# A two-layer matrix product by Strassen's scheme: block 0's second product moved ahead of block 1's first, partial outputs fetched from GpSimd's queue into output tiles, and a looped fallback

## The chip, the cores and the metric

The kernel runs on one core of one Trainium2 chip. The metric is device time in microseconds (us). The five engines of the core are named as the profile names them: PE (TensorE, the matrix products; PEld is its weight load), DVE (VectorE), ACT (ScalarE), POOL (GpSimd) and SP (SyncE). Each runs its own list of instructions in order and waits on semaphores for the others. SP, ACT and POOL issue DMAs: SP's go to hardware queue q1, ACT's to q10, POOL's to the software queue q0. All of them share 16 DMA engines.

## What is computed

```python
batch, m, k, h, n = 16, 512, 768, 3072, 768
y = np.matmul(x, w1) + b1        # x: 8192 rows of 768; w1: 768 x 3072
y = np.maximum(y, 0)
return np.matmul(y, w2)          # w2: 3072 x 768
```

All inputs and the output are float32 in DRAM.

## The kernel before

**Tiling.** The 8192 rows are cut into NSB = 8 blocks of 1024 rows, and the 3072 hidden columns into NCH = 2 halves. That gives NIT = 16 blocks of work, `it` = 0 to 15: blocks 0 to 7 are all rows with the first half of the hidden columns, blocks 8 to 15 all rows again with the second half. Each block has a first product (x times w1, bias, ReLU, giving y in f16) and a second product (y times w2). Both are done by Strassen's scheme in Winograd's form: seven products of half size instead of eight, on operands that are sums of quarters. DVE forms these sums: `sums_x` (three instructions, L230, L233, L237), `sums_w` (four, L190), `sums_y` (three, L291, L293, L295). Block 0's first product alone is done plainly (`first_plain`), since the sums of x and w1 do not exist yet.

**Groups and steps.** The work is a list of groups that is written by hand in `run` and then sorted by a key, so that the steps of neighbouring groups alternate. A group ("p1", 0, t) is block 0's plain first product for hidden tile t, four steps of six matmuls. A group ("m1", it, t) is the first product of block `it` for tile t of six: seven steps p1, p2, p6, p5, p7, p3, p4 of three matmuls of 128x512 (L336). A group ("m2", it, j) is the second product for 128-row tile j of four: seven steps of the same names, six matmuls of 128x384 each (L413). In a group the accumulator `a` is used on and on: step p6 adds onto it after ACT or DVE has copied it, p4 after DVE has taken p7 (L346 and L418 are the additions on DVE, L342 and L424 the copies on ACT).

Before the change the list is: block 0's six p1 groups; then for each block, the first two m1 groups of the next block, the four m2 groups of this one, and the last four m1 groups of the next. So two m1 groups of block 1 stand ahead of block 0's first m2 group.

**What hangs on the steps.** After each step `after` issues side work: loads of x and weights, transposes, sums, squares for a range check, saves to DRAM and fetches from it. Since every engine runs in program order, the place in this list is the place in each engine's queue. But an instruction is held only by its own engine's earlier ones and by its own data: a DMA hooked to a late step can start early when its queue is empty and its data are ready.

**x.** Block 0's rows come as float32 in eight DMAs from SP and ACT (`load_x_first`, L260), are turned on PE (L270) and copied to f16 by DVE and ACT (L277, L275). Later blocks come as f16 from POOL (`load_x`, L210) in two halves into the two buffers of the pool `raw`, are turned by DMA transposes on SP (`transpose_x`, L216), summed on DVE, and saved with their sums to DRAM (`save_x`, L240, 2688 KB) for blocks 8 to 15, which fetch them (`fetch_x`, L244). ACT squares the raw rows for the check (`square_x`, L222) and writes the squares over the rows. The tile of x has two buffers, so block 2's x takes the place of block 0's.

**Weights.** w1 comes by L172 and w2 by L179, both on POOL. `first_plain` sums each w1 tile at once. The six w2 tiles are summed in p1 groups 4 and 5 and in the first two m1 groups of block 1. The second half of w2 is loaded, summed and saved one tile a block in blocks 0 to 5.

**Output.** Blocks 0 to 7 store partial outputs; blocks 8 to 15 fetch them (`fetch_part`, L398, on SP, into a tile `pr` of the pool `raw`), add them and store again (L460 and L465, on SP). The two row halves of a group go to separate tiles `o1` and `o2`, two buffers each.

**Range check and fallback.** `out_of_range` (L486 to L512) reduces the squares to one count after block 11, which every engine reads into a register at once. At the end a branch (L669) skips `general_path`, a plain version of the whole computation, written out in full.

Of the kernel before, what the change touches and what calls it, by code (L numbers as in the profile page):

```python
# [27 lines left out]
def general_path(ctx, tc, xf, w1, b1, w2, of):  # L28

    nc = tc.nc  # L30
    M, K = xf.shape
    H, N = w2.shape
    KS, HS, MB = K // P, H // P, 512
# [7 lines left out]
    nc.sync.dma_start(out=b1_sb, in_=b1.rearrange("(t p) -> p t", p=P))  # L41
    nc.gpsimd.dma_start(out=w1_sb, in_=w1.rearrange("(t p) h -> p t h", p=P))
    nc.gpsimd.dma_start(out=w2_sb, in_=w2.rearrange("(t p) n -> p t n", p=P))
    xl_pool = ctx.enter_context(tc.tile_pool(name="gxl", bufs=2))
    xt_pool = ctx.enter_context(tc.tile_pool(name="gxt", bufs=2))
    yt_pool = ctx.enter_context(tc.tile_pool(name="gyt", bufs=2))
    o_pool = ctx.enter_context(tc.tile_pool(name="go", bufs=4))
    ps_t = ctx.enter_context(tc.tile_pool(name="gpt", bufs=2, space=PSUM))
    ps_1 = ctx.enter_context(tc.tile_pool(name="gp1", bufs=2, space=PSUM))
    ps_2 = ctx.enter_context(tc.tile_pool(name="gp2", bufs=4, space=PSUM))  # L50
    for m0 in range(0, M, MB):
        xt = xt_pool.tile([P, KS, MB], BF16, name="gxt")
        for r in range(0, MB, P):
            xl = xl_pool.tile([P, K], BF16, name="gxl")
            nc.gpsimd.dma_start(out=xl, in_=xf[m0 + r:m0 + r + P, :])
            pt = ps_t.tile([P, KS, P], BF16, name="gpt")
            for k in range(KS):
                nc.tensor.transpose(pt[:, k, :], xl[:, k * P:(k + 1) * P], ident)
            nc.vector.tensor_copy(out=xt[:, :, r:r + P], in_=pt)
        yt = yt_pool.tile([P, HS, MB], BF16, name="gyt")  # L60
        for h in range(HS):
            ps = ps_1.tile([P, MB], FP32, name="gp1")
# [3 lines left out]
            nc.scalar.activation(out=yt[:, h, :], in_=ps, func=ACTF.Relu,  # L66
                                 bias=b1_sb[:, h:h + 1])
        for r in range(0, MB, P):
            o = o_pool.tile([P, N], FP32, name="go")
            for j in range(2):  # L70
                ps = ps_2.tile([P, NF], FP32, name="gp2")
                for h in range(HS):
                    nc.tensor.matmul(ps, lhsT=yt[:, h, r:r + P],
                                     rhs=w2_sb[:, h, j * NF:(j + 1) * NF],
                                     start=(h == 0), stop=(h == HS - 1))
                nc.vector.tensor_copy(out=o[:, j * NF:(j + 1) * NF], in_=ps)
            nc.sync.dma_start(out=of[m0 + r:m0 + r + P, :], in_=o)


class Strassen:  # L80
# [66 lines left out]
    def constants(self):  # L147
        nc = self.nc
        HS = self.H // P
        self.ident = self.const.tile([P, P], FP32, name="ident")  # L150
        make_identity(nc, self.ident)
        self.b1_sb = self.const.tile([P, HS], FP32, name="b1_sb")
        self.b1y = self.const.tile([P, HS], FP32, name="b1y")

        self.xstat = self.const.tile([P, self.M // P], FP32, name="xstat")
        self.w1stat = self.const.tile([P, self.NCH * self.TP], FP32, name="w1stat")
        self.w2stat = self.const.tile([P, self.NCH * self.TP], FP32, name="w2stat")

    def bias(self):
        nc = self.nc  # L160
        nc.sync.dma_start(out=self.b1_sb, in_=self.b1.rearrange("(t p) -> p t", p=P))
        nc.vector.tensor_scalar(out=self.b1y, in0=self.b1_sb, scalar1=YS, scalar2=None,
                                op0=ALU.mult)

# [21 lines left out]

    def sums_w(self, w):
        for o, i, j in ((self.T3, self.B12, self.B22), (self.T1, self.B12, self.B11),
                        (self.T2, self.B22, self.T1), (self.T4, self.B21, self.T2)):
            self.nc.vector.tensor_tensor(out=w[:, o], in0=w[:, i], in1=w[:, j],  # L190
                                         op=ALU.subtract)

    def stat_w(self, stat, c, t, w):

        i = c * self.TP + t
# [3 lines left out]
                                  accum_out=stat[:, i:i + 1])  # L199
# [5 lines left out]
    def load_x(self, it):  # L205
        m0 = it * 2 * self.MH
        for half in range(2):
# [11 lines left out]
    def square_x(self, it, half, s, rows=None):  # L219
        i = (it * 2 + half) * 4 + s  # L220
        rows = self.raw[half][:, s, :] if rows is None else rows
        self.nc.scalar.activation(out=rows, in_=rows, func=ACTF.Square,  # L222
                                  accum_out=self.xstat[:, i:i + 1])
# [22 lines left out]
    def load_x_first(self):  # L246

        self.first_rows = []
        for half in range(2):
            if half == 0:  # L250
                tiles = [self.o_pool.tile([P, 1, self.N], FP32, name="xf", tag=f"o{1 + s // 2}")
                         for s in range(4)]
            else:
                two = [self.raw_pool.tile([P, 2, self.N], FP32, name="xf", tag="raw")
                       for _ in range(2)]
                tiles = [two[s // 2][:, s % 2:s % 2 + 1] for s in range(4)]
            for s, xr in enumerate(tiles):
                r = half * self.MH + s * P
                q = self.nc.sync if s % 2 else self.nc.scalar
                q.dma_start(out=xr[:, 0, :], in_=self.xf[r:r + P, :])  # L260
                self.first_rows.append(xr[:, 0, :])

    def transpose_x_first(self, half):
        nc = self.nc
        for s in range(4):
            rows = self.first_rows[half * 4 + s]
            for a in range(2):
                ps = (self.pa, self.pc)[a].tile([P, 3, P], FP32, name="ac"[a], tag="ac"[a])
                for k in range(3):
                    nc.tensor.transpose(ps[:, k, :],  # L270
                                        rows[:, (3 * a + k) * P:(3 * a + k + 1) * P],
                                        self.ident)
# [24 lines left out]
    def first_plain(self, t):  # L297
# [96 lines left out]
    def fetch_part(self, it, j):  # L394

        pr = self.raw_pool.tile([P, 2, self.N], FP32, name="pr", tag="raw")
        for half in range(2):
            self.nc.sync.dma_start(out=pr[:, half, :], in_=self.rows_of(it, j, half))  # L398
        self.part[it, j] = pr

    def second(self, it, j):
# [5 lines left out]
        pr = self.part.pop((it, j), None)  # L407
# [13 lines left out]
        def take(o, ps, half, col):  # L421

            if pr is None:
                nc.scalar.activation(out=o, in_=ps, func=ACTF.Copy, scale=inv)  # L424
            else:
                add(o, ps, pr[:, half, col * NH:(col + 1) * NH])

        def copy(name, ps, half, col):
            g[name] = self.s_tile(name)[:, 0:NH]
            take(g[name], ps, half, col)  # L430

# [5 lines left out]
        def p2():  # L437
            g["b"] = self.pb.tile([P, self.MH], FP32, name="b")[:, 0:NH]
            mm(g["b"], self.A12, self.B21, True)
            g["o1"] = self.o_pool.tile([P, self.N], FP32, name="o1")  # L440
            add(g["o1"][:, 0:NH], g["b"], g["s1"])
# [10 lines left out]
        def p7():  # L452
            mm(g["a"], self.S3, self.T3, False)
            g["o2"] = self.o_pool.tile([P, self.N], FP32, name="o2")
            add(g["o2"][:, NH:], g["a"], g["s5"])

        def p3():
            mm(g["c"], self.S4, self.B22, False)
            add(g["o1"][:, NH:], g["c"], g["s2"])
            nc.sync.dma_start(out=self.rows_of(it, j, 0), in_=g["o1"])  # L460

        def p4():
            mm(g["a"], self.A22, self.T4, False)
            take(g["o2"][:, 0:NH], g["a"], 1, 0)
            nc.sync.dma_start(out=self.rows_of(it, j, 1), in_=g["o2"])  # L465

        return [p1, p2, p6, p5, p7, p3, p4]


    def out_of_range(self):  # L470
# [6 lines left out]
        nw = self.NCH * self.TP  # L477
        nx, nb = self.M // P, self.H // P
        ones = self.const.tile([P, P], FP32, name="ones")
        nc.vector.memset(ones, 1.0)  # L480
        n = 2 * nw + nx + nb
        ok = self.const.tile([P, n], FP32, name="ok")
        low = self.const.tile([P, n], FP32, name="low")
        val = self.const.tile([P, n], FP32, name="val")

        nc.vector.tensor_copy(out=val[:, 0:nw], in_=self.w1stat)  # L486
        nc.vector.tensor_copy(out=val[:, nw:2 * nw], in_=self.w2stat)
        nc.vector.tensor_copy(out=val[:, 2 * nw:2 * nw + nx], in_=self.xstat)
        nc.vector.tensor_tensor(out=val[:, 2 * nw + nx:], in0=self.b1_sb, in1=self.b1_sb,
                                op=ALU.mult)  # L490
        ps = self.pb.tile([P, self.MH], FP32, name="b")
        nc.tensor.matmul(ps[:, 0:2 * nw], lhsT=ones, rhs=val[:, 0:2 * nw], start=True,
                         stop=True)
        nc.vector.tensor_copy(out=val[:, 0:2 * nw], in_=ps[:, 0:2 * nw])
        at = 0
        for width, hi, lo in ((nw, W1_HI, W1_LO), (nw, W2_HI, W2_LO), (nx, X_HI, X_LO),
                              (nb, B_HI, 0.0)):
            v = val[:, at:at + width]
# [203 lines left out]
```

## Time and profile before

| what | value |
|---|---|
| runs | 968.33, 970.03, 971.53 us; median 970.03 |
| profiled execution, its own time | 971.14 us |
| its span in the profile | 969.3 us |
| mean granted clock of PE | 0.978 |
| busy: PE, DVE, ACT, POOL | 899.5, 598.2, 407.2, 47.6 us |
| moved by DMA | 163.35 MB, mean 169 GB/s |
| HBM read, written | 95.37 MB, 76.48 MB |

The span is cut into 40 slices of 24.2 us for the digits of the page. A line of waits reads: who waited, for whom, the total in us, how many times, the longest. A line of a timeline reads: start and duration in us, engine, line, operation, what it writes and reads, its shape, how many were merged, and in brackets the idle time before it and what ended that. A line of a group ends in: busy us, mean ns of one, idle us before, and who ended most of that. A line of stretches reads: the stretch, its length, then busy us and instructions of each engine that has any, the granted clock, the share of the DMA engines and their GB/s. PE's matmuls are pipelined: the next starts before the one before it ends, so the work is counted by their spacing.

### The profile page before, as it was taken

Reading aid. Unit: us, or ns where it says so; the run is one execution under the profiler, and the core shown is the slowest. Engines: PE = TensorE matmul, PEld = TensorE weight load, DVE = VectorE, ACT = ScalarE, POOL = GpSimd, SP = SyncE. Lnnn points to the kernel's source line nnn. Section 1 sums busy time; section 2 is a strip of 40 time slices with the busy share of each in tenths; the row PEclk is TensorE's granted clock in tenths of the full one; section 3 lists DMA queues with packets and bytes.
Section 4 is the critical chain, followed back from the end, with each engine's and each line's share of the span. In section 5 each row is a group of like instructions: output and inputs, shape, how many; then the busy total and the mean of one; then the engine's idle time right before and its main releaser. Section 6 shows DMA issues by size and latency. Waiting matters only on the chain. (4 is left out here: it accounts for less than half of the span.)

```text
span 969.3 us, 12976 instructions
## 1 busy us (share of the span) xinstructions
PE 899.5 (93%) x4774; PEld 472.6 (49%) x4774; DVE 598.2 (62%) x1114; ACT 407.2 (42%) x697; POOL 47.6 (5%) x68
## 2 busy tenths in 40 slices
PE   4926999999999999999999999999998999998995
PEld 2502545545454555545454545545454554544543
DVE  0519276584857566583856768485765848576563
ACT  1733447758555545553525136153502405041220
POOL 4220000100000000010200000000000000000000
PEclk9968899999999999999999999999999999999998
DMA  9395895785858594754837443534443245331514
GB/s 228 57 189 162 222 289 109 211 188 131 254 128 261 108 309 97 242 155 126 165 113 291 189 180 131 214 145 163 149 181 144 114 180 191 134 131 66 195 49 151
DMA packets 113528, 163.35 MB, mean 169 GB/s; under 512 B 70960, under 2 KB 84272, under 8 KB 111408
## 3 DMA queue, kind: packets, MB, share of 16 engines
q1 hardware_dynamic: 80144, 140.41, 41.9%
q0 software_dynamic: 32736, 20.45, 15.7%
q10 hardware_dynamic: 576, 1.57, 0.4%
q8 instruction: 39, 0.64, 0.3%
q14 instruction: 33, 0.27, 0.1%
HBM read 95.37 MB, written 76.48 MB: 177 GB/s over the span
## 5 line engine op out<-in xcount | busy, mean ns | idle before, releaser
L413 PEld LDWEIGHTS <-y 128*128 128x128 f16 x2688 | 264.2, 98 | 205.2 <-issue 23.0
L336 PEld LDWEIGHTS <-w1s 128*128 128x128 f16 x1890 | 186.0, 98 | 226.9 <-issue 18.2
L413 PE MATMUL a<-w2s,y 128*128 128x384 f16 x1536 | 278.3, 328 | 18.7 <-DVE s L418 11.1
L336 PE MATMUL a<-x,w1s 128*128 128x512 f16 x1080 | 270.9, 382 | 5.7 <-ACT s L342 4.3
L342 ACT ACTIVATE s<-a,b1y 128x512 f32<-128x512 f32 x180 | 123.7, 687 | 332.6 <-PE a L336 326.5
L336 PE MATMUL c<-x,w1s 128*128 128x512 f16 x540 | 146.6, 380 | 0.9 <-DVE flag L510 0.7
L413 PE MATMUL c<-w2s,y 128*128 128x384 f16 x768 | 147.3, 328 | 0.0
L418 DVE SCALAR_TENSOR_TENSOR o<-a,s 128x384 f32<-128x384 f32 x64 | 35.4, 553 | 84.8 <-PE a L413 60.7
L346 DVE SCALAR_TENSOR_TENSOR y<-a,s 128x512 f16<-128x512 f32 x90 | 61.6, 684 | 35.9 <-ACT s L342 31.9
L291 DVE TENSOR_TENSOR y<-y 128x512 f16<-128x512 f16 x96 | 40.8, 425 | 63.3 <-ACT y L380 53.3
L380 ACT ACTIVATE y<-a,b1y 128x512 f16<-128x512 f32 x90 | 61.8, 687 | 31.9 <-PE a L336 31.9
L336 PE MATMUL b<-x,w1s 128*128 128x512 f16 x270 | 73.5, 381 | 0.0
L413 PE MATMUL b<-w2s,y 128*128 128x384 f16 x384 | 72.9, 326 | 0.0
L418 DVE SCALAR_TENSOR_TENSOR s<-a,pr 128x384 f32<-128x384 f32 x64 | 35.3, 551 | 57.7 <-DMA pr<-out_dram 50.0
L293 DVE TENSOR_TENSOR y<-y 128x1024 f16<-128x1024 f16 x96 | 66.4, 692 | 3.3
L342 ACT ACTIVATE s<-c,b1y 128x512 f32<-128x512 f32 x90 | 61.8, 687 | 12.9 <-PE c L336 12.9
L424 ACT ACTIVATE s<-a 128x384 f32<-128x384 f32 x64 | 31.2, 487 | 78.4 <-PE a L413 73.7
L346 DVE SCALAR_TENSOR_TENSOR y<-b,s 128x512 f16<-128x512 f32 x90 | 61.5, 684 | 2.5 <-PE b L336 1.6
L346 DVE SCALAR_TENSOR_TENSOR y<-c,s 128x512 f16<-128x512 f32 x90 | 61.3, 681 | 0.5
L222 ACT ACTIVATE xn<-xn 128x768 f16<-128x768 f16 x56 | 46.8, 837 | 22.9 <-DMA x<-xn 22.8
L375 DVE TENSOR_SCALAR y<-y 128x1536 f16<-128x1536 f16 x90 | 50.4, 560 | 3.1
L418 DVE SCALAR_TENSOR_TENSOR o<-b,s 128x384 f32<-128x384 f32 x64 | 35.4, 553 | 20.3 <-PE b L413 10.2
(59 smaller groups left out, 413.4 us busy)
## 6 DMA issues: line engine op xcount, KB each, us to landing
out_dram<-o SPq DMA_DIRECT2D x128, 384.0 KB, 2.6
pr<-out_dram SPq DMA_DIRECT2D x64, 384.0 KB, 4.1
xd<-x SPq DMA_DIRECT2D x8, 2688.0 KB, 12.6
x<-xd SPq DMA_DIRECT2D x8, 2688.0 KB, 9.3
xn<-in_x_dram POOLq DMA_DIRECT2D x14, 768.0 KB, 10.2
w1s<-in_w_dram POOLq DMA_DIRECT2D x24, 192.0 KB, 8.3
w2d<-w2t SPq DMA_DIRECT2D x6, 672.0 KB, 6.3
w2s<-w2d SPq DMA_DIRECT2D x6, 672.0 KB, 7.3
```

What stands on the lines that cost most here:

```text
L222: self.nc.scalar.activation(out=rows, in_=rows, func=ACTF.Square, accum_out=self.xstat[:, i:i + 1])
L291: tt(out=y[:, self.S1], in0=y[:, self.A21], in1=y[:, self.A22], op=ALU.add)
L293: tt(out=y[:, self.S3:self.S2 + 1:self.S2 - self.S3], in0=y[:, self.A21:self.S1 + 1], in1=a11, op=ALU.subtract)
L336: nc.tensor.matmul(ps, lhsT=w[:, slot, k, :], rhs=x[:, xslot, k, :], start=(start and k == 0), stop=(k == 2), skip_group_check=True)
L342: nc.scalar.activation(out=g[name], in_=ps, func=ACTF.Identity, bias=bias, scale=YS)
L346: nc.vector.scalar_tensor_tensor(out=y[:, slot], in0=ps, scalar=YS, in1=g[s], op0=ALU.mult, op1=ALU.add)
L375: nc.vector.tensor_scalar(out=y[:, 0:3], in0=y[:, 0:3], scalar1=0.0, scalar2=None, op0=ALU.max)
L380: nc.scalar.activation(out=y[:, self.A21], in_=g["a"], func=ACTF.Relu, bias=bias1, scale=YS)
L413: nc.tensor.matmul(ps, lhsT=ys[t][:, op, j * P:(j + 1) * P], rhs=ws[t][:, slot, :], start=(start and t == 0), stop=(t == self.TP - 1), ski ...
L418: nc.vector.scalar_tensor_tensor(out=o, in0=ps, scalar=inv, in1=s, op0=ALU.mult, op1=ALU.add)
L424: nc.scalar.activation(out=o, in_=ps, func=ACTF.Copy, scale=inv)
```

## The change

**Order.** The list begins: six p1 groups; m2 groups 0, 1, 2 of block 0; m1 groups 0, 1, 2 of block 1; m2 group 3 of block 0; m1 groups 3, 4, 5 of block 1. From block 1 on it is as before.

**Start.** Four float32 DMAs bring half 0 of block 0's x, into the two output tiles; half 1 comes as f16 from POOL and is turned on PE with an f16 identity. The bias comes as 24 contiguous rows on ACT's queue and is turned on PE after half 0 of x, and not by a DMA of single elements. POOL loads in the order w1 tiles 0 and 1, half 1 of x, w1 tiles 2 to 5, all of w2, half 0 of block 1's x.

**Hooks.** `after` becomes a table, `plan`. w2's sums go into p1 groups 3 to 5, w1's from `first_plain` into block 0's m2 groups. Block 1's x is turned and summed beside block 0's m2 groups, block 2's x is loaded, turned and summed beside m2 group 3 of block 0. Squares go to a tile of their own and no longer over the rows. The second half of w2 is prepared in blocks 1 to 6 rather than 0 to 5.

**Output.** A group has one output tile of both row halves. In blocks 8 to 15 the partial output is fetched by POOL straight into this tile, part n of 32 hooked three groups ahead, alternately in a buffer of the output pool and one of `raw`. The last group stores its second row half in two column halves.

**Check and fallback.** `out_of_range` runs in three stages within block 11, with the bounds written by POOL at the start. `general_path` becomes a loop over 128-row tiles with its DMAs on POOL.

The diff, cut to its core:

```diff
 def general_path(ctx, tc, xf, w1, b1, w2, of):
...
-    for m0 in range(0, M, MB):
...
+    with tc.For_i(0, M, P) as m0:
+        nc.gpsimd.dma_start(out=xl, in_=xf[bass.ds(m0, P), :])
...
     def bias(self):
...
-        nc.sync.dma_start(out=self.b1_sb, in_=self.b1.rearrange("(t p) -> p t", p=P))
-        nc.vector.tensor_scalar(out=self.b1y, in0=self.b1_sb, scalar1=YS, scalar2=None,
...
+        rows = self.const.tile([nb, P], FP32, name="b1_rows")
+        nc.scalar.dma_start(out=rows, in_=self.b1.rearrange("(t p) -> t p", p=P))
+        return rows
+
+    def turn_bias(self, rows):
...
+        ps = self.pb.tile([P, self.MH], FP32, name="b")
+        nc.tensor.transpose(ps[:, 0:nb], rows, self.ident[0:nb, 0:nb])
+        nc.vector.tensor_scalar(out=self.b1y, in0=ps[:, 0:nb], scalar1=YS, scalar2=None,
                                 op0=ALU.mult)
...
     def load_x_first(self):
...
+        for i in range(2):
+            o = self.o_pool.tile([P, 2, self.N], FP32, name="o")
+            for s in range(2):
+                r = (2 * i + s) * P
+                (self.nc.sync, self.nc.scalar)[s].dma_start(out=o[:, s, :],
+                                                            in_=self.xf[r:r + P, :])
+                self.first_rows.append(o[:, s, :])
...
-            self.sums_w(w)
...
+    def fetch_part(self, n):
+        it, j = self.NSB + n // 4, n % 4
+        pool = (self.o_pool, self.raw_pool)[n % 2]
+        o = pool.tile([P, 2, self.N], FP32, name="o", tag=("o", "raw")[n % 2])
         for half in range(2):
-            self.nc.sync.dma_start(out=pr[:, half, :], in_=self.rows_of(it, j, half))
-        self.part[it, j] = pr
+            self.nc.gpsimd.dma_start(out=o[:, half, :], in_=self.rows_of(it, j, half))
+        self.part[it, j] = o
...
-        pr = self.part.pop((it, j), None)
+        part = self.part.pop((it, j), None)
+        o = part if part is not None else self.o_pool.tile([P, 2, self.N], FP32, name="o")
...
     def run(self):
...
+        self.load_x_first()
+        rows = self.bias()
         self.load_w1(0, 0)
         self.constants()
-        self.load_x_first()
-        self.bias()
-        for t in range(1, TP):
+        self.load_w1(0, 1)
+        self.load_x(0, (1,))
+        for t in range(2, TP):
             self.load_w1(0, t)
+        for t in range(TP):
+            self.load_w2(self.new_w2(t), 0, t)
+        self.load_x(1, (0,))
...
         groups = [("p1", 0, t) for t in range(TP)]
-        for it in range(NIT):
+        groups += [("m2", 0, j) for j in range(3)]
+        groups += [("m1", 1, t) for t in range(3)]
+        groups += [("m2", 0, 3)]
+        groups += [("m1", 1, t) for t in range(3, TP)]
+        for it in range(1, NIT):
...
+    def plan(self):
...
+        put("p1", 0, 3, 3, self.load_x, 1, (1,))
+        for t, at in enumerate(((3, 3), (4, 1), (4, 2), (4, 3), (5, 1), (5, 3))):
+            put("p1", 0, *at, lambda t: self.sums_w(self.w2s[t]), t)
+        first_sums(0, "m2", 0, 0, (1, 3, 5))
+        put("m2", 0, 0, 0, self.new_x, 1)
+        put("m2", 0, 0, 0, self.transpose_x, 1, 0)
+        put("m2", 0, 0, 4, self.transpose_x, 1, 1)
+        for t, at in enumerate(((0, 6), (1, 1), (1, 3), (1, 5), (2, 1), (3, 0))):
+            put("m2", 0, *at, lambda t: self.sums_w(self.w1s[t]), t)
...
+        first_sums(1, "m2", 0, 2, (0, 2, 4))
+        put("m2", 0, 1, 6, self.load_x, 2, (0,))
+        put("m2", 0, 2, 6, self.load_x, 2, (1,))
+        put("m1", 1, 0, 1, self.new_x, 2)
+        put("m1", 1, 0, 1, self.transpose_x, 2, 0)
+        put("m1", 1, 1, 1, self.transpose_x, 2, 1)
+        first_sums(2, "m2", 0, 3, (1, 3, 5))
...
+        for n in range(4 * NSB):
+            if n < 2:
+                put("m2", NSB - 1, 3, 6, self.fetch_part, n)
+            elif n == 2:
+                put("m1", NSB, 2, 0, self.fetch_part, n)
+            else:
+                put("m2", NSB + (n - 3) // 4, (n - 3) % 4, 5, self.fetch_part, n)
+        for stage, at in enumerate(((0, 0), (1, 3), (3, 3))):
+            put("m2", NSB + 3, *at, self.out_of_range, stage)
```

Here `put(kind, it, q, i, fn, ...)` hooks a call to step i of a group, and `first_sums(it, kind, at, q, steps)` hooks the three sums of x of block `it` to these steps and its save to step 6 of the group.

More of the change, by code (lines that the diff above doesn't have):

```diff
@@ L65, in general_path @@
                                  rhs=xt[:, k, :], start=(k == 0), stop=(k == KS - 1))
[L66 to L77, printed above, removed]
+            nc.vector.tensor_scalar(out=yt[:, h, :], in0=ps, scalar1=b1_sb[:, h:h + 1],
+                                    scalar2=0.0, op0=ALU.add, op1=ALU.max)
+        for j in range(2):
+            ps = psum.tile([P, NF], FP32, name="gp2", bufs=2)
+            for h in range(HS):
+                nc.tensor.matmul(ps, lhsT=yt[:, h, :], rhs=w2_sb[:, h, j * NF:(j + 1) * NF],
+                                 start=(h == 0), stop=(h == HS - 1))
+            nc.vector.tensor_copy(out=o[:, j * NF:(j + 1) * NF], in_=ps)
+        nc.gpsimd.dma_start(out=of[bass.ds(m0, P), :], in_=o)
 class Strassen:
@@ L157, in constants @@
-        self.w2stat = self.const.tile([P, self.NCH * self.TP], FP32, name="w2stat")
+        self.ident16 = self.const.tile([P, P], FP16, name="ident16")
+        nc.gpsimd.tensor_copy(out=self.ident16, in_=self.ident)
+        self.b1y = self.const.tile([P, nb], FP32, name="b1y")
+        n = self.nstat = 2 * nw + nx + nb
+        self.stat = self.const.tile([P, n], FP32, name="stat")
+        self.stat_at = {"w1": 0, "w2": nw, "x": 2 * nw}
+        self.ones = self.const.tile([P, P], FP32, name="ones")
@@ L439, in p2 @@
             mm(g["b"], self.A12, self.B21, True)
[L440 to L441 removed]
+            add(out(0, 0), g["b"], g["s1"])
         def p6():
@@ L453, in p7 @@
             mm(g["a"], self.S3, self.T3, False)
-            g["o2"] = self.o_pool.tile([P, self.N], FP32, name="o2")
-            add(g["o2"][:, NH:], g["a"], g["s5"])
+            add(out(1, 1), g["a"], g["s5"])
+            if last:
+                store(1, 1)
         def p3():
             mm(g["c"], self.S4, self.B22, False)
-            add(g["o1"][:, NH:], g["c"], g["s2"])
-            nc.sync.dma_start(out=self.rows_of(it, j, 0), in_=g["o1"])
+            add(out(0, 1), g["c"], g["s2"])
@@ new lines, in plan @@
+        for c in range(self.NCH):
+            for t in range(TP):
+                at = (t // 2, 1 + 3 * (t % 2))
+                put("m2", c * NSB + 1, *at, self.stat_w, "w1", c, t, self.w1s)
+                put("m2", c * NSB + 2, *at, self.stat_w, "w2", c, t, self.w2s)
+        for t in range(TP):
+            put("m1", NSB - 1, t, 6, self.load_w1, 1, t)
+            at = (NSB - 2, 3, (2, 5)[t]) if t < 2 else (NSB - 1, t - 2, 3)
+            put("m2", *at, lambda t: self.sums_w(self.w1s[t]), t)
+            put("m2", NSB - 1, 3, 6, self.fetch_w2, t)
```

299 lines of the change are left out of this document (123 added, 176 removed).

## Prediction

> **What bounds the kernel now.** I read the page first, then PE's waits, then PE's timeline at both ends and at the range check, and at last DVE and the DMA queues where the change puts work. The span, PE's busy tenths (page), and the totals of waits:
>
> ```profile
> span 969.3 us, 12976 instructions
> PE   4926999999999999999999999999998999998995
> ...
> DVE b1y L162 <- DMA b_sb<-in_b_dram: 16.9, 1, 16.9
> ...
> PE a L307 <- ACT y L309: 18.9, 1, 18.9
> ...
> ACT xn L222 <- DMA x<-xn: 22.8, 7, 9.4
> ...
> PE a L413 <- DVE w2s L190: 4.7, 1, 4.7
> ...
> DVE s L418 <- DMA pr<-out_dram: 50.0, 15, 5.1
> PE a L413 <- DVE s L418: 11.1, 16, 2.4
> ...
> SPq L669 <- SPq L669: 3.8, 3, 2.2
> ```
>
> PE sets the time wherever its tenths are 9; only what PE loses can be won. The holes are the first four slices (24.2 us each) and small dents later. PE's timeline over the start and the first stall shows their size:
>
> ```profile
> 5.38 0.88 PE L270 MATMUL a<-ident,xf 128*128 128x128 f32 x3 [5.38 <-DMA xf<-in_x_dram]
> ...
> 8.61 0.85 PE L270 MATMUL c<-ident,xf 128*128 128x128 f32 x3
> ...
> 19.15 2.42 PE L307 MATMUL a<-x,w1s 128*128 128x512 f16 x6
> ...
> 51.70 1.46 PE L307 MATMUL b<-x,w1s 128*128 128x512 f16 x6
> 72.02 2.72 PE L307 MATMUL a<-x,w1s 128*128 128x512 f16 x6 [18.86 <-ACT y L309]
> ```
>
> The first product starts at 19.15 although x began to be transposed at 5.38: DVE stood behind the bias load (16.9). The last step of block 0's first product waits 18.9, because ACT, in order, stands at squares (L222) that overwrite rows which DMA transposes still read. How much PE loses from there on is read from one stretch, 53 to 130 us, line by line (L307, L336, L413), with the spacing of matmuls taken from one run of twelve:
>
> ```profile
> 53.00:130.00 77.00, 2.88 (x7) 0.69 (x5) 0.78 0.83 188
> ...
> 53.00:130.00 77.00, 14.37 (x48) 5.22 (x48) 0.78 0.83 188
> ...
> 53.00:130.00 77.00, 30.70 (x159) 16.90 (x160) 0.78 0.83 188
> ...
> 771.41 2.11 PE L413 MATMUL a<-w2s,y 128*128 128x384 f16 x12
> ```
>
> Matmuls overlap by half: twelve of 0.33 us in 2.11 are 0.1625 apart, six of 0.38 in 1.46 are 0.216. So a step of the second product is 0.975 us of PE, one of the first product 0.648 (block 0: 1.295). The stretch holds 55 x 0.216 + 159 x 0.1625 = 37.7 us of work in 77.0: **39.3 us lost**, at a granted clock of 0.78 in its row.
>
> **Start.** The bias comes as 24 rows and is turned on PE after the eight transposes of half 0, so DVE's copies follow the transposes. Six transposes took 5.38 to 8.61 plus one, 0.65 each; eight end near 10.7, the copy after them adds 0.6: the first product at 11.3, **7.9 us earlier**. The weights must be there. Shares of two DMA queues from 5 to 10 us, and of the third alone from 17 to 24 us:
>
> ```profile
> q1 hardware_dynamic: 328, 0.91, 49.5%
> ...
> q0 software_dynamic: 265, 0.07, 13.2%
> ...
> q0 software_dynamic: 5024, 1.26, 182.1%
> ```
>
> While x's rows fill the hardware queues, the weights on q0 get 0.014 MB/us; alone they get 0.18. A hardware queue moves 0.18 MB/us and now carries two row tiles, not four: the first two tiles were there at 5.4, two more need 0.39/0.18 = 2.2, so q0 is alone from 7.6. Weight tile 0 (0.39 MB) is there at 9.8, tile 1 at 12.0, half 1 of x (0.79 MB) at 16.4; they are wanted at 11.3, 14.9 and 17.5 (four steps of 1.295 and 1.0 for the slow first one, 2.42 against 1.46). It fits by a little; bound: 2 us lost, or 1 won, since fp16 transposes have no row.
>
> The last step then runs in its turn: 19.15 to 53.1 held 23 steps; with the 24th (1.295) and 7.9 less, block 0's first product ends at **46.5**.
>
> **Block 0's second product, next.** It needs all of w2's sums, block 1's x does not come into it. Rows of DVE's groups, and one run of four w2 subtractions:
>
> ```profile
> L418 DVE SCALAR_TENSOR_TENSOR o<-a,s 128x384 f32<-128x384 f32 x64 | 35.4, 553 | 84.8 <-PE a L413 60.7 <-ACT s L424 24.1
> L346 DVE SCALAR_TENSOR_TENSOR y<-a,s 128x512 f16<-128x512 f32 x90 | 61.6, 684 | 35.9 <-ACT s L342 31.9 <-PE a L336 3.9
> L291 DVE TENSOR_TENSOR y<-y 128x512 f16<-128x512 f16 x96 | 40.8, 425 | 63.3 <-ACT y L380 53.3 <-ACT y L309 9.4 <-ACTq L669 0.4
> L293 DVE TENSOR_TENSOR y<-y 128x1024 f16<-128x1024 f16 x96 | 66.4, 692 | 3.3
> ...
> L233 DVE TENSOR_TENSOR x<-x 128x3072 f16<-128x3072 f16 x8 | 14.0, 1750 | 0.1
> L230 DVE TENSOR_TENSOR x<-x 128x1536 f16<-128x1536 f16 x8 | 7.6, 951 | 21.0 <-DMA x<-xn 20.9
> ...
> 47.94 1.58 DVE L190 TENSOR_TENSOR w1s<-w1s 128x384 f16<-128x384 f16 x4
> ...
> L222 ACT ACTIVATE xn<-xn 128x768 f16<-128x768 f16 x56 | 46.8, 837 | 22.9 <-DMA x<-xn 22.8
> ```
>
> Sums of y are 0.425 + 0.692 + 0.425 = 1.54 a tile, those of a weight tile 1.58. From step (3,3), which ends at 46.5 - 8 x 1.295 = 36.1, DVE has three of y and six of w2: 14.1 us. It begins near 38.5 (0.9 for the evacuation, and ACT is 1.5 behind, as eight squares of 0.837 go between evacuations in groups 2 and 3), so the last T2, one subtraction before the end, is there at 52.2. PE wants it in the third step at 46.5 + 2 x 0.975 + 5 x 0.1625 = 49.3: **2.9 lost** (bounds 0 and 4.5). Hook for hook, DVE then trails PE by up to 2 us in groups 0 to 2; I put 0.4 on that. This stretch also takes the place of the 4.7 wait for w2s, which goes with the old order.
>
> **A new wait, at block 2's x.** The order on SP from here is: transposes of block 1, stores of groups 0 and 1 with the save of block 0's x between, transposes of block 2's half 0, stores of group 2, save of block 1's x, transposes of half 1. What it costs to stand behind a save: landing times of all saves (min/median/max), the two stores that were issued 1.6 and 3.2 us after a save in block 2 and their landing, and the time that transposes take to issue:
>
> ```profile
> DMA to landing us min/median/max: 7.8/9.9/15.0
> ...
> L460 SPq DMA_DIRECT2D out_dram<-o x1: 333/333/333, 185.9 to 185.9; - x1
> ...
> DMA to landing us min/median/max: 15.5/15.7/16.0
> ...
> L216 SPq DMA_TRANSPOSE x<-xn x13: 1224/1364/4194, 46.4 to 109.5; - x13
> ```
>
> A store normally lands in 2.6; behind a save it took 15.5: the queue is first in, first out. Now the chain. Block 0's sums end near 59.8 on DVE (52.6, then three adds, three sums of x, one tile of w1, and waits for PE), its save lands at 68, and x of block 2, starved on q0 meanwhile, lands 0.79/0.18 = 4.4 later with its latency: 73. Its four transposes take 5.4 alone and, with half 1 loading beside them, about 8 (bounds 5.4 and 16.8 from the row): 81. The save of block 1 then holds the queue 7.8 to 9.9: 90; half 1's transposes land near **94.5** (bounds 91 and 99).
>
> DVE reaches the sum that needs them, hooked to step 1 of group 3, at 85: 46.5 + 3.3 lost + 23 steps of 0.975 + 19 of block 1's first product, 0.648 each, is 84.5, and the step's add takes 0.55. DVE stands there in order. Once released it has that sum (0.95), an add and a clamp of block 1 (0.68 + 0.6), sums of y (1.54), the next sum of x (1.75) and an add (0.55) before PE may run group 3's seventh step, which PE reaches after 4 x 0.975 + 5 x 0.648 more, at 91.6: ready at 94.5 + 6.1 = 100.6, **9.0 lost** (bounds 5.6 and 14). After 18.9 idle the first six matmuls took 2.72, not 1.46, and the next were slow too: **2.0** for the clock. Of the 39.3, 2.9 + 0.4 + 9.0 + 2.0 = 14.3 stay: **25.0 gained**.
>
> After that the order of blocks 1 to 15 is the old one. An output tile is now shared by both halves, so group j + 2 waits for both stores of group j; the second of them lands late only while a w2 tile is saved, and DVE waits in front of work that PE does not need at once; I put 0 on it, bound 3.
>
> **Range check.** PE's timeline around it:
>
> ```profile
> 735.34 1.14 PE L413 MATMUL a<-w2s,y 128*128 128x384 f16 x6
> 737.36 0.40 PE L492 MATMUL b<-val,ones 128*128 128x24 f32 x2 [0.89 <-DVE val L487]
> ...
> 740.58 0.81 PE L336 MATMUL c<-x,w1s 128*128 128x512 f16 x3 [0.75 <-DVE flag L510]
> ...
> 745.50 0.81 PE L336 MATMUL a<-x,w1s 128*128 128x512 f16 x3
> ```
>
> From 735.34 to 745.50, 10.16 us hold 6 x 0.1625 + 15 x 0.216 = 4.2 of work: 5.9 lost, the slow clock after it included. Split over three places, PE still does two small products (0.4 each) and reads the flag (0.56): 1.3. **4.6 gained.**
>
> **Partial outputs.** PE waited 11.1 in 16 for DVE's additions of fetched parts, which waited for landings; those fetches stood on SP behind stores that wait for DVE. On Pool nothing stands before them but the release of the tile of part n - 4, a whole block earlier. I take **10.4**, keeping one mean wait (bounds 5 and 11.1).
>
> **Tail.** The last store's issue, and what the page says of stores:
>
> ```profile
> 960.56 0.33 SPq L465 DMA_DIRECT2D out_dram<-o  x1
> ...
> out_dram<-o SPq DMA_DIRECT2D x128, 384.0 KB, 2.6
> ```
>
> The end is 8.7 after that issue, 2.2 of it one wait on SP between its own branches (L669). The looped fallback leaves SP few instructions to jump over, and the last store is half as large: 2.2 + 0.6 = **2.8** (bounds 0 and 4). The Trainium skill (Runtime: NRT & Kernel Launch, Instruction fetch mechanics) says that a taken branch to code outside the window already fetched must wait for a fetch. By it the sum would keep the 2.2 if the looped body still lies outside the window, and end at 921.5; no run here shows a short jump.
>
> **Sum.** 7.9 + 25.0 + 4.6 + 10.4 + 2.8 = 50.7. The profiled execution took 971.14, its span and 1.84 around it: 920.4. The median of the runs is 1.11 lower: 919.3, forecast **919**.
>
> **Rivals.** First: the transposes of block 2 land in time (the queue lets them pass the save, or DVE reaches the sum later). Then 9.0 + 2.0 go too: 908.3. The rows of stores behind a save speak against it, that all its times are sums of estimates speaks for it. Chance 0.18.
>
> Second: DVE becomes the bound between 46 and 101. Its work there is 12 x 0.553 + 3 x 3.65 (x) + 6 x 1.58 (w1) + 6 x (3 x 0.684 + 0.6 + 1.54) = 52.2 us beside 54.5 of PE. If its waits in order keep it to 85%, it needs 61.4, and the loss grows by about 8: 927. Chance 0.15.
>
> Third: fetching on Pool changes nothing, as its own waits for released tiles come as late: 10.4 back, 930. Against it: the release is a block earlier. Chance 0.05.
>
> Fourth, the slow side: Pool is kept from writing its descriptors while DVE runs, and the front waits for 25 loads in a row up to the last w2 piece. The row of such loads, Pool's groups:
>
> ```profile
> L179 POOL DMA_DIRECT2D w2s<-in_w_dram x12 | 8.4, 702 | 6.0 <-DMA xn<-in_x_dram 3.5 <-DMA w2s<-in_w_dram 2.5
> ```
>
> It is slower than now when the last piece comes 53 us late, near 103: at 4.0 us a load, not 0.70. These twelve were issued from 42 to 56 while DVE did its f16 sums (row at 47.94), at 0.70. The Trainium skill (SBUF — State Buffer, SBUF: two separate sides) states the lockout for DVE's two-port modes and advises the hardware queues instead; the trace does not show it here. At 4.5 us a load the last comes at 114, 64 after PE wants it, and the time is about 983. Chance 0.02.
>
> **Numbers.** Forecast 0.60, rivals 0.18, 0.15, 0.05, 0.02. With its bounds the forecast alone runs from 911 to 929; the first two rivals lie at 908.3 and 927, so 906 to 931 holds a little over 8 in 10. A measurement here tells 0.3% (2.9 us) from no change. Faster 0.97, within it 0.01, slower 0.02.
>
> **What would show it.** Right: the first L307 product near 11.3; no wait for L309; a PE wait of about 3 for w2s; DVE's L230 sum in one wait of about 9 for DMA x<-xn, followed by half-speed matmuls; PE's waits for part additions under 2 in all; less than 2 lost near the flag; an end 6 us after the last store. Wrong: a first product after 14, a second PE stall elsewhere before 110, or part waits still near 11.

## The result and the profile after

| | before | changed |
|---|---|---|
| median of 4 runs each | 969.18 us | 919.71 us |
| lowest to highest | 967.53 to 971.53 | 918.58 to 920.73 |
| profiled execution, its span | 971.14, 969.3 | 918.58, 917.0 |
| mean granted clock of PE | 0.978 | 0.99 |

The ratio is 0.9488, with a 95% interval of 0.9463 to 0.9512. The forecast was 919. The total hides that single terms missed in both directions, by up to 8.6 us, and nearly cancelled.

The page of the changed kernel, its span and PE's busy tenths (slices of 22.9 us now):

```profile
span 917.0 us, 13090 instructions
...
PE   7997499999999999999999999999999999999997
```

Before, the first slice was a 4 and the third and fourth were 2 and 6 (of 24.2 us); one hole is left now, in slices four and five. PE's timeline of the changed kernel at the start, at the end of block 0's first product, and around that hole:

```profile
5.24 0.87 PE L295 MATMUL a<-ident,o 128*128 128x128 f32 x3 [5.24 <-DMA o<-in_x_dram]
...
8.92 0.49 PE L295 MATMUL c<-ident,o 128*128 128x128 f32 x3
...
9.74 1.46 PE L331 MATMUL a<-x,w1s 128*128 128x512 f16 x6 [0.16 <-DVE x L301]
...
16.53 0.33 PE L295 MATMUL c<-ident,xn 128*128 128x128 f16 x3
...
43.04 1.14 PE L440 MATMUL a<-w2s,y 128*128 128x384 f16 x6
...
85.78 0.81 PE L359 MATMUL a<-x,w1s 128*128 128x512 f16 x3
104.19 2.08 PE L440 MATMUL a<-w2s,y 128*128 128x384 f16 x6 [17.61 <-DVE o L445]
106.07 1.29 PE L359 MATMUL c<-x,w1s 128*128 128x512 f16 x3
```

The first product starts at 9.74 (19.15 before), at full speed at once. The second product of block 0 begins at 43.04. Then PE stands for 17.6 us in front of the seventh step of group 3, the place that the prediction named. DVE's timeline of the changed kernel shows why PE stands there:

```profile
80.54 0.55 DVE L445 SCALAR_TENSOR_TENSOR o<-b,s 128x384 f32<-128x384 f32 x1
98.13 0.96 DVE L260 TENSOR_TENSOR x<-x 128x1536 f16<-128x1536 f16 x1 [17.05 <-DMA x<-xn]
...
103.59 0.55 DVE L445 SCALAR_TENSOR_TENSOR o<-a,s 128x384 f32<-128x384 f32 x1
```

After the add of step 1 DVE waits 17.05 for the transposes of block 2's x, works off what stood behind it, and makes the addition that PE needs from 103.59 on. PE's other waits after the first product's start that are longer than 0.3 us (list of waits, then the groups of the range check, which end in busy us, mean ns and idle us before them):

```profile
PE a L440 <- DVE w2s L219: 1.4, 1, 1.4
...
PE a L440 <- DVE s L445: 0.9, 1, 0.9
...
PE a L359 <- DVE y L369: 0.8, 1, 0.8
...
L516 PE MATMUL b<-stat,ones 128*128 128x24 f32 x2 | 0.3, 228 | 0.0
L526 PE MATMUL b<-good,ones 128*128 128x1 f32 x2 | 0.3, 209 | 0.0
```

The wait for w2s went from 4.7 to 1.4, the waits for additions of parts from 11.1 in 16 to 0.9 in one, and the range check stops PE no more. The end comes 5.6 us after PE's last matmul; it was 9.3.

### The profile page after: what moved, and what is told of

The parts are those of the page before. It is cut to its first block, busy times and chain, and to the rows that moved or that the text cites. A ratio compares the mean times of both kernels' runs of the same rounds, so it can differ in the third digit from the quotient of the medians.

```text
span 917.0 us, 13090 instructions
## 1 busy us (share of the span) xinstructions
PE 884.6 (96%) x4775; PEld 467.8 (51%) x4775; DVE 601.9 (66%) x1103; ACT 407.7 (44%) x698; POOL 84.0 (9%) x143
## 5 line engine op out<-in xcount | busy, mean ns | idle before, releaser
L440 PE MATMUL a<-w2s,y 128*128 128x384 f16 x1536 | 277.3, 327 | 20.0 <-DVE o L445 17.6
L359 PE MATMUL a<-x,w1s 128*128 128x512 f16 x1080 | 267.8, 380 | 0.8 <-DVE y L369 0.8
L424 POOL DMA_DIRECT2D o<-out_dram x64 | 34.6, 546 | 388.4 <-DMA out_dram<-o 167.5
L252 ACT ACTIVATE junk<-xn 128x768 f16<-128x768 f16 x60 | 50.4, 840 | 0.3
```

What stands on the lines that cost most here:

```text
L252: self.nc.scalar.activation(out=junk[:, 0:2].rearrange("p a n -> p (a n)"), in_=rows, func=ACTF.Square, accum_out=self.stat[:, i:i + 1])
L359: nc.tensor.matmul(ps, lhsT=w[:, slot, k, :], rhs=x[:, xslot, k, :], start=(start and k == 0), stop=(k == 2), skip_group_check=True)
L424: self.nc.gpsimd.dma_start(out=o[:, half, :], in_=self.rows_of(it, j, half))
L440: nc.tensor.matmul(ps, lhsT=ys[t][:, op, j * P:(j + 1) * P], rhs=ws[t][:, slot, :], start=(start and t == 0), stop=(t == self.TP - 1), ski ...
```

## The experiments

### The save behind the transposes

```diff
-        first_sums(1, "m2", 0, 2, (0, 2, 4))
+        for n, i in enumerate((0, 2, 4)):
+            put("m2", 0, 2, i, self.sums_x, 1, n)
...
         put("m1", 1, 1, 1, self.transpose_x, 2, 1)
+        put("m1", 1, 1, 2, self.save_x, 1)
```

> One hook is moved: the save of block 1's x is issued on SP after the transposes of half 1 of block 2's x, and not ahead of them. Theory (the stall of 17.6 us in front of group 3's seventh step is the landing of these transposes, which stand in SP's queue behind a save of 2688 KB): they are issued from 79 us as now but land near 85, not 98; DVE's first sum of block 2's x starts there, its chain of 6.1 us lets PE go on near 91 instead of 104.2, and part of the slow clock after the stall goes too: 13 to 15 us less than the changed kernel's 919.7, about 905 to 907. Rival (DVE's own work is the bound between 46 and 101 us, and the transposes only hide it): under 5 us gained, 915 to 920, with DVE without a gap where it waits now.

Measured: 908.33 us, 11.4 less. DVE's one wait, the four transposes' issue and their landing, first in the changed kernel, then in this one. The landing line (min/median/max) covers what loads or turns x between 78.8 and 91.3 us; its 11.7 in the second is block 3's load:

```profile
DVE x L260 <- DMA x<-xn: 17.1, 1, 17.1
...
L245 SPq DMA_TRANSPOSE x<-xn x4: 1813/2464/4524, 79.4 to 89.0; - x4
...
DMA to landing us min/median/max: 8.2/10.0/10.9
```

```profile
DVE x L260 <- DMA x<-xn: 5.3, 1, 5.3
...
L245 SPq DMA_TRANSPOSE x<-xn x4: 1286/1294/1687, 79.1 to 83.5; - x4
...
DMA to landing us min/median/max: 2.8/2.8/11.7
...
PE a L440 <- DVE o L445: 5.9, 1, 5.9
```

The first is issued at the same moment (79.1 against 79.4), but the four go out by 84.8 instead of 90.8 and land 2.8 us after issue instead of 8 to 11; PE's stall is 5.9, not 17.6. So moving the save takes away 11.8 of DVE's 17.1. The gain in time, 11.4, is 1.6 less than the low end expected: PE goes on at 92.6, not near 91, and the idle time of 5.9 is still followed by slow matmuls. No other wait took the place, so the rival falls. What the run does not tell apart is standing behind the save in SP's queue and sharing the DMA engines with it: the save on another queue was not tried. In the changed kernel the save lands at 88.3 and the first two transposes right after it, at 89.2 and 90.0, which speaks for the queue.

### The load beside the transposes

```diff
-            put("m2", 0, 3, i, self.square_x, 2, 0, s)
+            put("m1", 1, 4, i, self.square_x, 2, 0, s)
```

> The squares of half 0 of block 2's x move from block 0's group 3 to block 1's first-product group 4, so that the tile is released later and the load of block 3's x, which starts at 86.9 us now, cannot run beside the last transposes of block 2. Theory of two causes (first two of the four late transposes landed at 89.2 and 90.0, right behind the save, the other two at 97 beside that load): all four land near 91.5, the stall shrinks by 6 to 7 us, about 913. Rival (the load alone delays them): they land near 85 and 12 or more is gained, under 908. Rival (the save alone does): nothing changes, 919 to 920.

Measured: 914.68 us, 5.0 less. DVE's wait and the transposes in this kernel:

```profile
DVE x L260 <- DMA x<-xn: 11.5, 1, 11.5
...
L245 SPq DMA_TRANSPOSE x<-xn x4: 1527/2499/4530, 79.5 to 89.1; - x4
```

The wait is 5.6 shorter, though the transposes are issued as before. So there were two causes in a row: the save, and then the load of block 3's x, which in the changed kernel was let go at 86.86 us, between the third transpose (86.4) and the fourth (89.0), and here starts at 106. Of the 17.1, 5.3 stay without the save; of the other 11.8, 5.6 go with the load alone and 6.2 are the save's own. Moving the save takes both, since the transposes then land before the load starts (87.0). The second cause is not in the prediction. Neither rival holds.

### The fallback written out

The looped `general_path` is replaced by the long one; nothing else.

> The changed kernel with the fallback written out in full, as before. Theory: at the end SP and DVE must again wait for a fetch when they jump over it (2.3 us on SP in the kernel before, 0.1 now), but PE's own jump takes 4.1 us in both and ends 2 us after the last store has landed, which covers a part: 1.0 to 1.5 us slower, about 921. Rival (SP's jump counts in full): 2.2 or more, 922. Rival (PE's jump covers it all): no difference, under 0.5.

Measured: 920.85 us, 1.1 more, with the changed kernel's runs at 918.58 to 920.73 and these at 920.11 to 921.70: at the edge of what times can tell. The traces bear it out: from PE's last matmul to the end it is 6.9 us here and 5.6 in the changed kernel. SP's waits for itself, in this kernel:

```profile
SPq L700 <- SPq L700: 3.2, 2, 1.7
```

The profile puts 3.2 us on SP itself, and none in the changed kernel. But the longer of these waits ends at 916.7, when the last store lands (issued at 913.1, landing after 3.6), and in the changed kernel SP waits for that landing as well (1.9, to 915.7). What differs is the time from the landing to the end: 2.6 us here, 1.3 there. PE's jump over the fallback took 4.2 here and 4.1 there; in the changed kernel it ends at 915.8, together with the landing, and not 2 us behind it as was expected.

### The fetch on SP

```diff
-            self.nc.gpsimd.dma_start(out=o[:, half, :], in_=self.rows_of(it, j, half))
+            self.nc.sync.dma_start(out=o[:, half, :], in_=self.rows_of(it, j, half))
```

> The changed kernel with the 64 fetches of partial outputs issued on SP instead of Pool, at the same hooks and into the same tiles. Theory of the prediction (SP's order was the cause: a fetch stands behind stores that wait for DVE): PE's waits for additions of parts come back, about 10 us, 930. Rival (what counts is four tiles and a hook three groups ahead; before it was two tiles and one group): even on SP a fetch is issued about 10 us ahead of its use and lands in 4 to 5, so nothing is lost: 919 to 921.

Measured: 919.79 us, the same as with POOL (919.71), and PE's only wait for the addition of a part is the same 0.9 us:

```profile
PE a L440 <- DVE s L445: 0.9, 1, 0.9
```

The prediction's reason for this term, that fetches stood on SP behind stores, is refuted.

### The fetch on POOL in the kernel before

The same edit the other way in the kernel before: `fetch_part` on `nc.gpsimd`, still into two tiles of `raw` and at the old hooks.

> The kernel before with one edit: the 64 fetches of partial outputs are issued on Pool instead of SP, at the same hooks and into the same two tiles. Theory (after the run of the changed kernel with its fetches on SP, which was as fast: the lead is what counts; with two tiles, part 2 of a block can only be fetched when part 0 has been added, one step of the second product ahead of its use): PE's waits of 11.1 us for additions of parts stay at 8 or more, 966 to 971. Rival (the prediction's reason, SP's order): they fall under 3, about 960.

Measured: 976.89 us against 970.88, ratio 1.0059 (1.0040 to 1.0078): slower by 0.6%. PE's waits in this kernel and the landing of its fetches (min/median/max), then the landing of them in the kernel before:

```profile
PE a L413 <- DVE s L418: 18.5, 17, 1.4
...
DMA to landing us min/median/max: 3.4/4.5/11.7
```

```profile
DMA to landing us min/median/max: 3.2/4.1/12.4
```

The waits grow from 11.1 to 18.5. With two tiles, part 2 of a block waits for part 0 to be added, and is wanted a step or two later; its landing time lies open, and POOL's is the longer. So the lead, four tiles and a hook three groups ahead, brought the gain, and the queue alone is a loss that the lead hides. Tiles and hook were not taken apart.

### The range check at one place

```diff
-        for stage, at in enumerate(((0, 0), (1, 3), (3, 3))):
+        for stage, at in enumerate(((3, 6), (3, 6), (3, 6))):
```

> The changed kernel with the three stages of the range check at one place, after block 11's last step, as before. Theory: PE waits there for DVE's part and for the flag again and runs at a lower clock after it; with fewer DVE instructions than before (4 for 12) 4 to 5 us are lost instead of none: 924. Rival (what stopped PE before was the work on the bounds, which Pool now does at the start): under 2 us, 921.

Measured: 923.90 us, 4.2 more. PE's timeline there:

```profile
700.62 1.14 PE L440 MATMUL a<-w2s,y 128*128 128x384 f16 x6
701.60 0.30 PE L516 MATMUL b<-stat,ones 128*128 128x24 f32 x2
703.68 0.38 PE L526 MATMUL b<-good,ones 128*128 128x1 f32 x2 [1.78 <-DVE good L523]
705.08 1.44 PE L359 MATMUL c<-x,w1s 128*128 128x512 f16 x3 [1.02 <-DVE flag L529]
706.31 2.31 PE L359 MATMUL a<-x,w1s 128*128 128x512 f16 x6
```

PE waits again, 1.78 and 1.02 (before the change 0.89, 1.68 and 0.75), and behind these waits six matmuls take 2.31, not 1.46. The split is worth some 4 of the 5.9. The rest, by difference alone, would be POOL's work on the bounds.

### The bias by single elements

```diff
-        rows = self.const.tile([nb, P], FP32, name="b1_rows")
-        nc.scalar.dma_start(out=rows, in_=self.b1.rearrange("(t p) -> t p", p=P))
+        rows = self.const.tile([P, nb], FP32, name="b1_rows")
+        nc.sync.dma_start(out=rows, in_=self.b1.rearrange("(t p) -> p t", p=P))
+        nc.vector.tensor_scalar(out=self.b1y, in0=rows, scalar1=YS, scalar2=None, op0=ALU.mult)
```

It is issued after `constants`, and `turn_bias` keeps only the squares.

> The changed kernel with the bias loaded again by single elements on SP and scaled by DVE ahead of its copies of x. Theory: the first product starts near 14.5, not 9.7, because DVE stands behind that load (it lands near 12); the chain of loads that ends the stall of 17.6 us is itself let go by steps of the products, so it moves along and the loss reaches the end: 3 to 5 us slower, 923 to 925. Rival (the stall ends at a time set by DMAs alone and takes the late start in): under 1 us, 920.

Measured: 925.32 us, 5.6 more. PE's timeline of this kernel at the start:

```profile
13.55 0.90 PE L292 MATMUL a<-ident,o 128*128 128x128 f32 x3 [3.85 <-DVE x L298]
14.25 0.85 PE L292 MATMUL c<-ident,o 128*128 128x128 f32 x3
15.10 2.67 PE L328 MATMUL a<-x,w1s 128*128 128x512 f16 x6
```

The first product starts 5.4 later, and slow. The stall at group 3 is the longer of two waits in one line of the list:

```profile
PE a L437 <- DVE o L442: 17.9, 2, 17.6
```

It is as long as in the changed kernel (17.6), though PE reaches it 6.2 later: its DMA chain moved with the products. So the bias's form is worth over half of the 9.4 us at the start, and a time won ahead of such a stall is kept when the chain behind the stall hangs on the products.

### Squares apart in the kernel before

```diff
-        self.nc.scalar.activation(out=rows, in_=rows, func=ACTF.Square,
-                                  accum_out=self.xstat[:, i:i + 1])
+        junk = self.s_pool.tile([P, 4, self.NH], FP16, name="junk")
+        self.nc.scalar.activation(out=junk[:, 0:2].rearrange("p a n -> p (a n)"), in_=rows,
+                                  func=ACTF.Square, accum_out=self.xstat[:, i:i + 1])
```

> The kernel before with one edit: squares go to a tile of their own and no longer over the rows, so ACT does not wait for the DMA transposes. Theory (the hole from 53 to 74 us was not only ACT's: DVE waits for the same transposes until 70.4, and block 1's first product, next in the order, needs its sums at 73): the wait for L309 goes, but PE stops two steps later until 73, and 2 to 6 us are gained, 964 to 968. Rival (the 18.9 us were ACT's order alone): 15 or more gained, under 955, and then the new order of groups was not needed for it.

Measured: 972.54 us, ratio 1.0008 (0.9989 to 1.0027): no difference, less even than the 2 to 6 expected. PE's timeline in the hole of this kernel:

```profile
56.92 1.45 PE L308 MATMUL a<-x,w1s 128*128 128x512 f16 x6 [1.94 <-ACT y L310]
69.19 1.44 PE L337 MATMUL a<-x,w1s 128*128 128x512 f16 x3 [10.82 <-DMA x<-xn]
70.43 1.48 PE L337 MATMUL b<-x,w1s 128*128 128x512 f16 x3
76.75 1.46 PE L337 MATMUL a<-x,w1s 128*128 128x512 f16 x3 [4.84 <-DVE x L234]
```

PE's wait of 18.9 for ACT is gone (1.94 is left), and PE waits for the same transposes itself (10.82) and then for their sums (4.84). The line that ended the wait in the profile before was not the limit; the arrival of block 1's x was, and the new order, which does not need it yet, is what takes this hole away.

### The faster versions

The save as in the first experiment, and the sums of block 2's x in block 1's first-product groups 3 to 5:

```diff
-        first_sums(2, "m2", 0, 3, (1, 3, 5))
+        for n, at in enumerate(((3, 4), (4, 4), (5, 3))):
+            put("m1", 1, *at, self.sums_x, 2, n)
+        put("m1", 1, 5, 6, self.save_x, 2)
```

> The save moved as in the experiment before it, and the three sums of block 2's x with their save moved from block 0's group 3 to block 1's first-product groups 3, 4 and 5. Theory: DVE reaches the first of them after the transposes have landed (86.4 in that experiment), so PE is not stopped: the 8.3 us that PE still lost between 75 and 100 us go, about 900. Rival (DVE is nearly full in these first-product groups, 4.15 us of work in 4.5 of PE, so the added sums stop PE there instead): 2 to 4 us are lost again, 902 to 905.

Measured: 901.70 us, ratio to the kernel before 0.9289 (0.9261 to 0.9318). PE's waits in it:

```profile
PE a L359 <- DVE y L369: 2.2, 2, 1.5
PE a L440 <- DVE w2s L219: 1.4, 1, 1.4
PE a L440 <- DVE s L445: 0.9, 1, 0.9
```

The stall is gone; a wait of 1.5 for DVE in block 1 is the price, so the rival has a small part. Last, w2's sums hooked earlier as well, at ((2, 3), (3, 1), (3, 3), (4, 1), (4, 3), (5, 1)):

> The fastest version so far (save after the transposes, sums of block 2's x late), with the six sums of w2 hooked three to four steps earlier, from group 2 of block 0's first product on. Theory: w2 has landed by 36.6 us and DVE has room in groups 2 to 4, so the last T2 is there before PE wants it at 45.9 and the 1.4 us wait for w2s goes: 900.3, a step that is at the edge of what the times can tell. Rival (sums of y of the last groups set it, not w2's): no difference, 901.7.

Measured: 900.27 us (899.92 to 900.72; the version before 901.39 to 902.14), ratio to the kernel before 0.9271 (0.9251 to 0.9292). The wait for w2s is no longer in PE's list. This is the fastest version, 7.3% under the kernel before and 19.4 us under the change.

## Why the prediction was right

By its own steps, from the profiled executions, in us:

| step | forecast | measured |
|---|---|---|
| end of block 0's first product | 46.5, 7.9 gained | 43.04, 11.4 gained |
| wait for w2's sums | 2.9 | 1.4 |
| DVE behind PE in groups 0 to 2 | 0.4 | no wait |
| stall at group 3 | 9.0 | 17.6 |
| slow matmuls after it | 2.0 | 1.4 |
| range check, gained | 4.6 | 5.9 |
| part waits, gained | 10.4 | 10.2 |
| tail, gained | 2.8 | 3.8 |
| span, gained | 50.7 | 52.3 |

**The total: luck in part.** With the 39.3 lost before in the stretch from 53 us, the measured rows add up to 50.2; the other 2.1 of the 52.3 lie in none of them and stay open. The stall cost 8.6 more than forecast, and the start (3.5), w2's sums (1.5), the check (1.3), the tail (1.0) and smaller terms gained nearly as much more. Nothing ties these misses together, so that they cancel is luck. The range was narrower than its own bounds: all at once, they would give 910 to 939, not 911 to 929.

**Start: mechanism right, size small.** The bias form is shown by its run. The rest of the miss is in rows: the last transposes of half 0 are 0.33 apart and not 0.65, the first six matmuls of the product take 1.46 and not 2.42, and half 1 in f16 is turned in 1.5 us (15.35 to 16.86), so that the product goes on 2.2 after it left off (14.9 to 17.14), where the prediction kept the 3.1 of the kernel before (25.29 to 28.40). The first of these is partly chance: in the profile of the fastest version, whose start is the same, all transposes of half 0 are 0.64 apart and the first product starts at 10.98, nearer the 11.3 of the forecast.

**The stall: right place, one cause of two, mis-sized.** The term "the transposes of half 1 land near 94.5, PE reaches the step at 91.6, 9.0 lost" should have read: the last of them lands at 98.1, PE is there at 86.6, 17.6 lost, above the bound of 14. DVE's work behind the landing took the 6.1 forecast. The save landed at 88.3 (forecast 90) and the first two transposes right behind it; the last two came late beside the load of block 3's x, which the chain of the prediction does not hold and which is worth 5.6 of the wait by its own run. That PE came 5.0 earlier did not by itself lengthen the stall: with the start 5.4 later it is the same 17.6, because the chain hangs on the products. Counted from the end of block 0's first product, the transposes landed 7.1 later than forecast (55.1 against 48.0) and PE reached the step 1.6 earlier (43.5 against 45.1).

**The part waits: right size, wrong reason.** "Those fetches stood on SP behind stores that wait for DVE" failed twice: on SP the changed kernel is as fast, and on POOL the kernel before is slower. The prediction did name the release of a tile as what a fetch waits for, but only for the new kernel; it held for the old one too, with two tiles.

**The hole from 53 us.** The prediction put the 18.9 on ACT's squares; taken away alone they gain nothing. The price of the whole stretch, counted as work against time, was right without that reason.

**Check and tail.** The split leaves PE no loss at all: the two small products show no idle time before them, and the register read, 0.49 us on PE's sequencer, passes while matmuls are queued; the prediction charged 1.3. The tail's term named the right thing, but read the wrong wait for it. The 2.2 of SP ends at 964.7, when the last store, issued at 960.6 and landing after 4.1, is there. What the change took away stands behind the landing: from it to the end it was 4.6 us (2.3 of them SP's own last jump, from its branch at 965.3 to its next instruction at 967.6), and is 1.3 now. With the fallback written out again 1.1 us come back, half of the 2.2; why SP's last jump takes 0.4 in that run and not the 2.3 of the kernel before stays open. The half store lands after 3.6, not 4.1: 0.5 of the 0.6. The Trainium skill's sentence on taken branches (Runtime: NRT & Kernel Launch, Instruction fetch mechanics) is that a taken branch out of the window already fetched has to wait for a fetch. The trace agrees as far as it goes, since it does not show the window: SP, with next to nothing to skip, jumps without a wait, and PE, with some 200 matmuls in the looped body, still takes 4.1 us.

The slow rival did not come: POOL's loads of w2 in the front took 0.70 to 0.71 us each, as before, with DVE at its f16 sums for a part of that time. The second rival, DVE as the bound, is refuted by the first experiment for the stall and has 1.5 us in the fastest versions.

## What to carry to other kernels

A wait in the profile names what ended it last, not what would end it next: take the wait away alone before a reorder is built on it, and ask what is late then. Count what stands ahead of a transfer in its queue and what runs beside it: here a save that nobody waits for cost 11.4 us. When a prefetch is late, first ask when its buffer comes free; here another queue changed nothing, or made it worse, while the buffer set the time.

## What was not expected of the hardware

- The same four DMA transposes, issued at the same places, landed 2.8 us after issue when nothing stood ahead of them, and 8 to 11 behind a save of 2688 KB that itself landed 9.6 us after issue, with a load beside the last two. Their issue grew as well, from 1.3 to 1.7 us each to 1.8 to 4.5.
- At the start the transposes got faster by themselves: groups of three f32 ones were 0.64 apart up to 7.8 us and 0.33 from 8.3 on, without a break in PE's work, while the granted clock's row reads 1.00 before and after. The moment differs between runs whose start is the same: in the fastest version it came only after all eight, near 11 us. In the kernel before it did not come ahead of PE's wait in two profiles, and came near 8 us in a third (the one with its fetches on POOL).
- A fetch of 384 KB on POOL landed after 4.5 us in the middle, on SP after 4.1; with no lead the kernel on POOL was 6 us slower over 32 parts.
- PE's idle times of 1.78 and 1.02 us, close together, were followed by six matmuls in 2.31 us and not 1.46; a single one of 1.4, and one of 2.45 in the kernel before (twelve in 2.11 behind it), were not followed by slow ones.
